# Two transformer blocks on one core: expert 0's first 512 inner columns for all tokens ahead of the routing, and a plan with four 64-row experts

## The chip, the cores and the metric

One core of a Trainium2 chip runs the whole program in one launch. The metric is the device time of one execution in microseconds, as the median of the runs; nothing is split over cores, so there is no slowest core to pick. The other quantities are those of one profiled execution.

## The reference

256 tokens of 1024 values go through two layers of one block and two of another, in float32. The part that matters here is the mixture of experts in the second layer of the first block:

```python
def moe_ffn(x, router_w, w1, w3, w2):
    logits = (xt @ router_w).astype(F32)                  # 256 x 8
    top_v, top_i = lax.top_k(logits, TOP_K)               # 2 of 8
    top_w = jax.nn.softmax(top_v, axis=-1)
    gates = jnp.sum(jax.nn.one_hot(top_i, N_EXPERTS, dtype=F32) * top_w[..., None], axis=1)
    for e in range(N_EXPERTS):
        y = y + gates[:, e:e + 1].astype(x.dtype) * swiglu(xt, w1[e], w3[e], w2[e])
```

`swiglu` is `(silu(x @ w1) * (x @ w3)) @ w2`, with 3584 inner columns for each expert. `x` is the output of a layer norm behind the projection `w_out` of the layer's mixer; behind the experts stands another layer norm with the residual `ALPHA * x`. The kernel computes an expert only for the tokens that were routed to it.

## The kernel before

**Weights.** Every weight comes in units of 1 MB, 128 partitions by 2048 values (`unit`, L169). SP issues the transfer into a tile `raw`; ScalarE writes the rounded high part `wh` and VectorE the rest `wl` (`split`, L165); TensorE multiplies high by high, high by low and low by high parts. There are four buffers each of `wh` and `wl`. `raw` has four of its own, and within the experts every third load takes one of the ten large buffers (`roomy`, L175).

**Routing.** `route` (L805) makes the logits, marks each token's two experts (`sel`), counts the tokens of each expert, sorts the experts by count into slots 0 to 7, and writes the experts' numbers, and a flag for the plan, as integers into `idi` (L883 to L889). SP reads the numbers from there, since they select the weights' addresses (L1154, L1233), and every engine reads the flag and branches (L1234 to L1239). Until then no expert's weight is fetched.

**Tiles.** The tokens of a slot are gathered by a product with a one-hot matrix into a tile `ring` (`place`, `gather`): 128 rows with high and low part in two halves, three matmuls for a product, or 64 rows with high and low part side by side in one stationary tile, two matmuls for a product. The plan `few` holds where slot 0 has at most 192 tokens, slot 1 at most 128 and slot 6 at most 64. It runs four groups: slot 0 with a 128-row and a 64-row tile together with slots 7 and 6 as 64-row tiles; slot 1; slots 2 and 3; slots 4 and 5. All of the last five have one 128-row tile.

**Steps.** An expert is done in seven steps f of 512 inner columns (`expert`, L931): two units of w1 and two of w3 (`up`), the product of the two (`gate`, `mul`), its transposition (`turn`), and two units of w2 (`down`). `phases` (L1160) writes the order by hand: in a step the experts of a round follow one another, and the `down` of an expert comes after the `up` of the next, so that `turn` has time. `stream` (L1068) issues the units two ahead of their use. The 128-row and two-tile experts sum over all seven steps in PSUM; the 64-row experts beside the two-tile expert, for which PSUM has no room, add each step's result to a tile `ysum` on VectorE (`add`, L1021). At the end `put_back` and `finish` bring the rows back to their tokens by a product with the transposed one-hot matrix (`sct`) and add them, times the gate, to the result (L1060). A 64-row gate takes ScalarE and VectorE in turn: a copy (L975), an add (L976), two activations (L977, L978).

**Order of instructions.** Each engine runs its own instructions in order. A scheduler sets that order when the program is built, from the order in which the code issues them and from what is ready; what stands inside a branch isn't mixed with what stands outside. In the projection ahead of the experts (`project`, L383) the last three units are run for token tile 0 and then for tile 1, and the layer norm of tile 0 (`post`) lies beside tile 1's products.

## Time and profile before

| | |
|---|---|
| median of 3 runs | 2357.88 us (2356.47 to 2361.75) |
| the profiled execution | 2355.55 us |
| its span, first to last instruction | 2353.8 us |
| TensorE busy | 2272.1 us, 97% of the span |
| VectorE busy | 1765.4 us, 75% |
| ScalarE busy | 1396.0 us, 59% |
| weight units of the experts | 336 transfers of 1024 KB |

A matmul is entered as busy until its modelled end, and the next one begins before that end; so a busy TensorE is a TensorE that was never without work, and the pace of its matmuls is read from their starts. The profile names the engines PE (TensorE; PEld are its weight loads), DVE (VectorE), ACT (ScalarE), POOL (GpSimd) and SP. `wl<-raw,wh` is VectorE's split of a unit, `wh<-raw` is ScalarE's, `lin` is the accumulator of w1 or w3, `y` that of w2, `uT` the transposed product, `ga` the gather.

### The profile page before, as it was taken

The numbers are of one execution on the slowest core, as the hardware profiler recorded it, in microseconds if no ns is written. First come the engines' busy times: TensorE is split into PE (matmuls) and PEld (weight loads), VectorE is DVE, ScalarE is ACT, GpSimd is POOL, SyncE is SP. The second block draws the span as 40 slices with busy tenths as digits, with TensorE's granted clock in tenths as the row PEclk, the third lists the DMA queues.
The fourth block names the chain that finished last, engine by engine and source line by source line (L and its number), as shares of the span: only waits on it lengthen the run. The fifth ranks groups of instructions, "written<-read, shape, count | busy, mean of one in ns | idle before, by whom it ended". The sixth has DMA issues, their size and how long they took to land. (4 is left out here: it accounts for less than half of the span.)

```text
span 2353.8 us, 29770 instructions
## 1 busy us (share of the span) xinstructions
PE 2272.1 (97%) x11444; PEld 1853.7 (79%) x11444; DVE 1765.4 (75%) x1907; ACT 1396.0 (59%) x1532; POOL 108.9 (5%) x154
## 2 busy tenths in 40 slices
PE   7999999799999989999999997999999999999998
PEld 6788887577777768888888886787888888888887
DVE  4665476798888998889888888897666459956653
ACT  5554354677777777676776765457555343764542
POOL 2100011000000000000000001000200001010000
PEclk9999999899999999999999999999999999999999
DMA  9556560699999999999999997643755553555552
GB/s 298 167 191 187 178 209 21 248 343 345 344 337 322 330 326 368 347 368 362 371 342 371 369 365 255 200 162 117 230 190 181 192 189 126 188 172 186 191 185 72
DMA packets 266968, 585.10 MB, mean 249 GB/s; under 512 B 10514, under 2 KB 21190, under 8 KB 266561
## 3 DMA queue, kind: packets, MB, share of 16 engines
q1 hardware_dynamic: 260880, 565.48, 68.4%
q0 software_dynamic: 5936, 17.64, 2.6%
q8 instruction: 91, 1.49, 0.3%
q14 instruction: 61, 0.49, 0.1%
HBM read 580.43 MB, written 2.64 MB: 248 GB/s over the span
## 5 line engine op out<-in xcount | busy, mean ns | idle before, releaser
L167 DVE TENSOR_TENSOR wl<-raw,wh 128x2048 fp32r<-128x2048 f32 (+2 forms) x532 | 1195.5, 2268 | 373.2 <-ACT wh L166 372.1
L166 ACT ACTIVATE wh<-raw 128x2048 fp32r<-128x2048 f32 (+2 forms) x532 | 990.2, 1891 | 383.8 <-PE lin L84 145.3
L950 PE MATMUL lin<-wh,ring 128*128 128x512 f32 x1680 | 556.0, 391 | 0.0
L950 PE MATMUL lin<-wl,ring 128*128 128x512 f32 (+1 forms) x1008 | 396.2, 393 | 3.7 <-DVE wl L167 3.3
L950 PEld LDWEIGHTS lin<-wh,ring 128*128 128x128 f32 x1680 | 315.4, 188 | 81.8
L950 PEld LDWEIGHTS lin<-wl,ring 128*128 128x128 f32 (+1 forms) x1008 | 171.4, 170 | 48.7 <-DVE wl L167 8.5
L84 PE MATMUL lin<-wh,hh 128*128 128x512 f32 x352 | 141.8, 403 | 0.0
L84 PE MATMUL lin<-wl,hh 128*128 128x512 f32 x352 | 138.4, 393 | 2.3 <-DVE wl L167 2.3
L84 PE MATMUL lin<-wh,hl 128*128 128x512 f32 x352 | 137.9, 393 | 0.1
L950 PE MATMUL y<-wl,uh 128*128 128x512 f32 x336 | 107.3, 400 | 3.4 <-DVE wl L167 3.4
L1442 DVE SCALAR_TENSOR_TENSOR ro<-conv,ro 128x256 f32<-128x256 f32 x240 | 105.4, 474 | 0.4
L950 PE MATMUL y<-wh,ul 128*128 128x512 f32 x336 | 104.2, 391 | 0.0
L950 PE MATMUL y<-wh,uh 128*128 128x512 f32 x336 | 104.1, 390 | 0.0
L84 PE MATMUL lin<-wh,h2h 128*128 128x512 f32 x256 | 101.1, 395 | 0.0
L84 PE MATMUL lin<-wl,h2h 128*128 128x512 f32 x256 | 99.9, 390 | 0.2
L84 PE MATMUL lin<-wh,h2l 128*128 128x512 f32 x256 | 99.3, 390 | 0.2
L84 PE MATMUL lin<-wh,xah 128*128 128x512 f32 (+1 forms) x240 | 87.4, 365 | 0.7 <-ACT xah L166 0.6
L84 PE MATMUL lin<-wl,xah 128*128 128x512 f32 (+1 forms) x240 | 86.6, 361 | 0.0
L84 PE MATMUL lin<-wh,xal 128*128 128x512 f32 (+1 forms) x240 | 86.4, 363 | 0.0
L166 ACT ACTIVATE uh<-uT 128x512 fp32r<-128x512 f32 x42 | 25.1, 598 | 99.3 <-PE uT L1004 99.3
L84 PEld LDWEIGHTS lin<-wl,hh 128*128 128x128 f32 x352 | 66.7, 190 | 16.1 <-DVE wl L167 3.2
L84 PEld LDWEIGHTS lin<-wh,hh 128*128 128x128 f32 x352 | 66.8, 190 | 15.6 <-issue 1.3
(548 smaller groups left out, 3812.5 us busy)
## 6 DMA issues: line engine op xcount, KB each, us to landing
raw<-in_moe_w SPq DMA_DIRECT2D x336, 1024.0 KB, 7.2
raw<-in_w_in SPq DMA_DIRECT2D x70, 1024.0 KB, 5.1
raw<-in_w_ff SPq DMA_DIRECT2D x64, 1024.0 KB, 5.2
raw<-in_ffn_w SPq DMA_DIRECT2D x32, 1024.0 KB, 5.1
raw<-in_w_out SPq DMA_DIRECT2D x12, 1024.0 KB, 8.0
raw<-in_w_branch SPq DMA_DIRECT2D x8, 1024.0 KB, 5.7
raw<-in_w_out SPq DMA_DIRECT2D x8, 512.0 KB, 7.4
raw<-in_w_branch SPq DMA_DIRECT2D x8, 512.0 KB, 6.3
```

Of the source, the lines that this page charges most:

```text
L84: nc.tensor.matmul(o, lhsT=lhsT, rhs=rhs, start=(self.i == 0 and self.fresh), stop=(self.i == self.n - 1), skip_group_check=True)
L166: self.nc.scalar.activation(h, src, AF.Copy)
L167: self.nc.vector.tensor_sub(l, src, h.bitcast(F32))
L950: nc.tensor.matmul(a.ap[:rows], lhsT=lhsT, rhs=u[part][:, kk, cs], start=(a.i == 0), stop=(a.i == a.n - 1), skip_group_check=True)
L1442: nc.vector.scalar_tensor_tensor(acc[:, f], uT[:, f, k:k + 256], cw[:, f, k:k + 1], acc[:, f], op0=OP.mult, op1=OP.add)
```

## The change

Expert 0 always gets slot 0 (1024 is added to its count before the sort). Its first step is done for all 256 tokens, without gathering (`everyone`): the first unit is issued within the projection (`hook`), and the products are issued between the parts of the routing, whose code is cut in two by a `yield`. The result is added to the output times expert 0's gate, which is 0 for tokens not routed to it. Expert 0's own round then has the six steps 1 to 6, on one 128-row tile, and the four w1 and w3 units of step 1 are issued ahead of the branch (`landed`). The raw tiles are a ring of six, four small ones and two of the large buffers.

There are three plans. `light` runs where slot 0 has at most 128 tokens, slot 1 at most 192, slot 2 at most 128, and slots 4 and 6 at most 64. Its groups are slot 0; slot 1 with two tiles together with slots 7, 6 and 5 as 64-row tiles (the third of their sums takes one raw tile of the ring until that expert is finished); slot 2; and slot 3 with 128 rows together with slot 4 with 64 rows, as two experts of one round, slot 4 summing in PSUM. `few` is what runs where only slot 4's limit fails.

```diff
@@ -166,19 +167,26 @@
+    def raw(self):
+        if self.raws:
+            self.raws.append(self.raws.pop(0))
+            return self.raws[-1]
+        return self.pw.tile([128, 2048], F32, tag="raw", name="raw")
...
-        self.loads += 1
-        raw = (self.big("raw") if self.roomy and self.loads % 3 == 0 else
-               self.pw.tile([128, 2048], F32, tag="raw", name="raw"))
+        there = bool(self.landed)
+        raw = self.landed.pop(0) if there else self.raw()
...
-        if layout == "rows":
+        if there:
+            pass
+        elif layout == "rows":
@@ -396,6 +404,8 @@
         self.warm(AF.Sqrt, x(orders[-1][-1], 1)[0])
         after = {t: (lambda t=t: post(t, [banks[0][t], banks[1][t]])) for t in range(2)}
         after[1, 1] = self.early
+        if self.hook:
+            after[0, 0] = self.hook
         yield from self.run_b(specs[cut:], x, tmajor=True, after=after)
@@ -761,15 +771,18 @@
+            if l == 1:
+                everyone = self.everyone(*(io[k][0, 0] for k in ("moe_w1", "moe_w3", "moe_w2")))
+                self.hook = everyone["first"]
             xt, tr1 = self.ln_out(self.mix1(l, xt, tr1), io["ln1_g"][l], io["ln1_b"][l])
+            self.hook = None
...
-                tr1()
-                self.moe(xt, io["router_w"][0], io["moe_w1"][0], io["moe_w3"][0], io["moe_w2"][0],
+                self.moe(xt, tr1, everyone, io["router_w"][0], io["moe_w1"][0], io["moe_w3"][0], io["moe_w2"][0],
                          io["ln2_g"][l], io["ln2_b"][l])
@@ -851,6 +864,7 @@
             nc.vector.tensor_scalar(sel[:, 8 * t:8 * t + 8], rank[:, 8 * t:8 * t + 8], 1.5, None, op0=OP.is_lt)
+        yield
         pc = self.bank("cum")
@@ -860,8 +874,11 @@
+        key = col(8)
+        nc.vector.tensor_copy(key, cnt)
+        nc.vector.tensor_scalar(key[:, 0:1], cnt[:, 0:1], 1024.0, None, op0=OP.add)
+        mine = key[:, :, None].to_broadcast([128, 8, 8])
+        other = key[:, None, :].to_broadcast([128, 8, 8])
...
+        most = (self.cap, self.cap + 64, self.cap, 64)
+        for i, (slot, m) in enumerate(zip((0, 1, 2, 6), most)):
+            if i == 0:
+                nc.vector.tensor_scalar(fit[:, 0:1], cs[:, 0:1], m + 0.5, None, op0=OP.is_lt)
+            else:
+                nc.vector.tensor_scalar(fit[:, i:i + 1], cs[:, slot:slot + 1], m + 0.5, fit[:, i - 1:i], op0=OP.is_lt,
+                                        op1=OP.mult)
+        nc.vector.tensor_scalar(fit[:, 4:5], cs[:, 4:5], 64.5, fit[:, 3:4], op0=OP.is_lt, op1=OP.mult)
+        nc.vector.tensor_add(fit[:, 5:6], fit[:, 3:4], fit[:, 4:5])
+        nc.vector.tensor_copy(idi[:, 16:17], fit[:, 5:6])
@@ -1012,8 +1035,8 @@
-                        if q == 0 and (f == 0 or inner):
-                            st[i]["y"] = [Acc(self.bank("y"), (4 if inner else 28) * per[i]) for c in range(2)]
+                        if q == 0 and (f == first or inner):
+                            st[i]["y"] = [Acc(self.bank("y"), (4 if inner else 28 - 4 * first) * per[i]) for c in range(2)]
@@ -1086,16 +1110,89 @@
+    def everyone(self, w1, w3, w2):
+
+        nc = self.nc
+        w = {"a": w1, "b": w3}
+        u, p, s, y, xt = {}, {}, {}, {}, []
+
+        def load(name, q):
+            u[name, q] = self.unit(w[name], list(range(4 * q, 4 * q + 4)), 0, 512)
+
+        def up(name, t):
+            x = self.xt_tok(xt)
+            p[name, t] = Acc(self.bank("lin"), 24)
+            for q in range(2):
+                h, l = u[name, q]
+                for kk in range(4):
+                    xh, xl = x(4 * q + kk, t)
+                    p[name, t].mm(nc, xh, h[:, kk])
+                    p[name, t].mm(nc, xh, l[:, kk])
+                    p[name, t].mm(nc, xl, h[:, kk])
+            if name == "a":
+                s[t] = self.mid("sa")
+                nc.scalar.activation(s[t], p[name, t].ap, AF.Silu)
+            else:
+                nc.vector.tensor_mul(s[t], s[t], p[name, t].ap)
+
+        def turn(t):
+            b = self.bank("uT")
+            for j in range(4):
+                nc.tensor.transpose(b[:, j * 128:(j + 1) * 128], s[t][:, j * 128:(j + 1) * 128], self.ident)
+            h, l = self.mid("uh", (128, 4, 128), dt=F32R), self.mid("ul", (128, 4, 128), dt=F32R)
+            self.split(h, l, b.rearrange("p (j c) -> p j c", c=128))
+            s[t] = h, l
+
+        def down(q):
+            h, l = self.unit(w2, [2 * q, 2 * q + 1], 0, 1024)
+            for t in range(2):
+                if q == 0:
...
+                    uh, ul = (z[:, 2 * q + kk] for z in s[t])
+                    for st, m in ((uh, h), (uh, l), (ul, h)):
+                        for c in range(2):
+                            y[t][c].mm(nc, st, m[:, kk, c * 512:(c + 1) * 512])
+
+        return dict(first=lambda: load("a", 0), load=load, up=up, turn=turn, down=down, y=y, xt=xt)
+
+    def moe(self, xt, tr1, everyone, rw, w1, w3, w2, g2, b2):
         tc, nc = self.tc, self.nc
-        gate, pos, iota, idi = self.route(xt, rw)
+        load, up, turn = (everyone[k] for k in ("load", "up", "turn"))
+        everyone["xt"].extend(xt)
+        self.raws = [*(self.raw() for _ in range(4)), self.big("raw"), self.big("raw")]
+        load("a", 1)
+        up("a", 0)
+        tr1()
+        route = self.route(xt, rw)
+        next(route)
+        load("b", 0)
+        load("b", 1)
+        up("b", 0)
+        up("a", 1)
+        gate, pos, iota, idi = next(route)
         xh = self.bigr("xh").rearrange("p (t d) -> p t d", d=D)
         xl = self.bigr("xl").rearrange("p (t d) -> p t d", d=D)
         acc = self.x
+        turn(0)
+        up("b", 1)
         for t in range(2):
             nc.scalar.activation(xh[:, t], acc[:, t], AF.Copy)
             nc.gpsimd.tensor_sub(xl[:, t], acc[:, t], xh[:, t].bitcast(F32))
             nc.scalar.activation(acc[:, t], acc[:, t], AF.Copy, scale=self.alpha)
+        turn(1)
+        for q in range(2):
+            everyone["down"](q)
+        for t in range(2):
+            for c in range(2):
+                o = acc[:, t, c * 512:(c + 1) * 512]
+                nc.vector.scalar_tensor_tensor(o, everyone["y"][t][c].ap, gate[t][:, 0:1], o, op0=OP.mult, op1=OP.add)
+        landed = []
+        for w in (w1, w3):
+            for q in range(2):
+                landed.append(self.raw())
+                nc.sync.dma_start(landed[-1].rearrange("p (k n) -> p k n", n=512),
+                                  w[0, 512 * q:512 * q + 512, 512:1024].rearrange("(k p) n -> p k n", p=128))
         ring = [self.bigr("ring") for _ in range(4)]
         ysum = self.big("ysum").rearrange("p (i d) -> p i d", d=D)
         for z in (*ring, ysum[:, 0], ysum[:, 1]):
@@ -1147,8 +1244,12 @@
             return tiles, lambda: self.gather(g, parts, xh, xl)
 
         index = {}
+        raws = list(self.raws)
+        sums = [ysum[:, 0], ysum[:, 1], raws[-1][:, 0:1024]]
 
         def weights(s):
+            if s == 0:
@@ -1163,7 +1264,7 @@
             for make, early, late in rounds:
                 es = make()
-                for f in range(7):
+                for f in range(es[0][5], 7):
                     for e in es:
                         jobs = e[0](f)
...
             yield call(e[4])
-            yield from e[1](6)
+            jobs = e[1](6)
+            yield jobs[0]
+            if done:
+                yield call(done[3])
+            yield from jobs[1:]
             yield call(e[3])
         def run(plan):
+            self.landed, self.raws = list(landed), list(raws)
...
                                 if inner is not None:
-                                    zs[0]["sum"] = ysum[:, inner]
-                                es.append(self.expert(zs, weights(s), acc))
+                                    zs[0]["sum"] = sums[inner]
+                                if inner == 2:
+
+                                    self.raws.remove(raws[-1])
+                                    zs[0]["free"] = lambda: self.raws.append(raws[-1])
+                                es.append(self.expert(zs, weights(s), acc, int(s == 0)))
@@ -1223,21 +1332,28 @@
-        few = [([(0, 0, False), (0, self.cap, True), (7, 0, True), (6, 0, True)],
-                [[(0, (0, 1), None), (7, (2,), 0), (6, (3,), 1)]])]
-        few += [([(1, 0, False)], [one(1)])]
-        few += [([(s, 0, False), (s + 1, 0, False)], [one(s), one(s + 1, 1)]) for s in (2, 4)]
-        many = [([(s, 0, False), (s, self.cap, False)], [[(s, (0, 1), None)]]) for s in range(3)]
-        many += [([(s, 0, False), (s + 1, 0, False)], [one(s), one(s + 1, 1)]) for s in (3, 5)]
-        many += [([(7, 0, False)], [one(7)])]
-        index[0] = nc.values_load(idi[0:1, 0:1], engines=[mybir.EngineType.SP], min_val=0, max_val=7)
-        n = nc.values_load(idi[0:1, 16:17], min_val=0, max_val=1)
-        self.roomy = True
-        with tc.If(n > 0) as cmp:
-            run(few)
+        light = [([(0, 0, False)], [one(0)]),
+                 ([(1, 0, False), (1, self.cap, True), (7, 0, True), (6, 0, True), (5, 0, True)],
+                  [[(1, (0, 1), None), (7, (2,), 0), (6, (3,), 1), (5, (4,), 2)]]),
+                 ([(2, 0, False)], [one(2)]),
+                 ([(3, 0, False), (4, 0, True)], [[(3, (0,), None), (4, (1,), None)]])]
+        few = [([(0, 0, False)], [one(0)]),
+               ([(1, 0, False), (1, self.cap, True), (7, 0, True), (6, 0, True)],
+                [[(1, (0, 1), None), (7, (2,), 0), (6, (3,), 1)]]),
+               ([(2, 0, False)], [one(2)]),
+               ([(3, 0, False), (4, 0, False)], [one(3), one(4, 1)]),
+               ([(5, 0, False)], [one(5)])]
+        many = [([(s, 0, False), (s, self.cap, False)], [[(s, (0, 1), None)]]) for s in range(4)]
+        many += [([(s, 0, False), (s + 1, 0, False)], [one(s), one(s + 1, 1)]) for s in (4, 6)]
+        n = nc.values_load(idi[0:1, 16:17], min_val=0, max_val=2)
+        with tc.If(n > 1) as cmp:
+            run(light)
         with cmp.Else():
-            run(many)
-        self.roomy = False
+            with tc.If(n > 0) as inner:
+                run(few)
+            with inner.Else():
+                run(many)
+        self.raws = []
```

## Rows read from the trace of the kernel before

**Rows 1.** The page, DMA in 40 slices of 58.8 us (busy tenths).

```profile
DMA  9556560699999999999999997643755553555552
```

**Rows 2.** Stretches: us, then busy us (instructions) of PE, PEld, DVE, ACT, POOL; clock, DMA share, GB/s.

```profile
547.95:603.37 55.42, 53.72 (x245) 39.66 (x245) 48.96 (x34) 40.73 (x33) 0.00 (x0) 1.00 0.97 342
...
1396.19:1412.97 16.78, 16.78 (x78) 13.87 (x77) 14.68 (x9) 12.01 (x9) 0.00 (x0) 1.00 1.01 371
```

**Rows 3.** Waits, 480 to 820 us: who waits for whom, total us, times, longest.

```profile
DVE wl L167 <- ACT wh L166: 29.8, 35, 1.8
...
PE y L950 <- DVE wl L167: 6.1, 14, 0.8
...
PE lin L950 <- DVE wl L167: 1.7, 4, 0.6
```

**Rows 4.** Waits, 840 to 1400 us.

```profile
ACT wh L166 <- PE lin L950: 10.5, 15, 2.5
...
PE lin L950 <- DVE wl L167: 1.0, 1, 1.0
```

**Rows 5.** Groups by line, VectorE, 547.95 to 603.37 us: busy us, mean ns, idle before.

```profile
L167 DVE TENSOR_TENSOR wl<-raw,wh 128x2048 fp32r<-128x2048 f32 x18 | 40.8, 2287 | 4.9 <-ACT wh L166 4.7
...
L1029 DVE TENSOR_TENSOR ysum<-ysum,y 128x512 f32<-128x512 f32 x5 | 3.2, 680 | 0.0
...
L985 DVE TENSOR_TENSOR sa<-sa,lin 128x512 f32<-128x512 f32 x4 | 2.7, 680 | 1.4 <-PE lin L950 1.4
...
L976 DVE TENSOR_TENSOR sa<-lin,sa 64x512 f32<-64x512 f32 x3 | 2.0, 682 | 0.1
...
L167 DVE TENSOR_TENSOR uhl<-uT,uhl 128x256 fp32r<-128x256 f32 x3 | 1.3, 419 | 0.1
```

**Rows 6.** Timeline of TensorE in one step of the two-tile round: start us, duration.

```profile
547.95 0.50 PE L950 MATMUL lin<-wl,ring 128*128 128x512 f32 x1 [0.38 <-DVE wl L167]
...
566.14 0.39 PE L950 MATMUL y<-wh,uhl 128*128 128x512 f32 x1
...
569.82 0.60 PE L1004 MATMUL uT<-ident,sa 128*128 128x128 f32 x4
...
571.10 0.47 PE L950 MATMUL lin<-wh,ring 128*128 128x512 f32 x1
...
578.59 0.62 PE L950 MATMUL y<-wh,uh 128*128 128x512 f32 x2
...
588.33 1.00 PE L997 MATMUL uT<-keep,sa 128*128 128x64 f32 x8
...
589.14 0.47 PE L950 MATMUL lin<-wh,ring 128*128 128x512 f32 x1
...
603.37 0.50 PE L950 MATMUL lin<-wl,ring 128*128 128x512 f32 x1 [0.37 <-DVE wl L167]
```

**Rows 7.** Timeline between projection and experts, TensorE and VectorE.

```profile
411.30 0.39 PE L84 MATMUL prj<-wh,yl 128*128 128x512 f32 x1
...
431.47 0.29 DVE L1124 TENSOR_SCALAR g<-keep 128x128 fp32r<-128x128 f32 x1 [0.52 <-DVE keep L879]
...
441.97 0.39 PE L950 MATMUL lin<-wh,ring 128*128 128x512 f32 x1
```

**Rows 8.** Stretches from the projection's end on.

```profile
411.90:424.20 12.30, 4.91 (x42) 4.34 (x42) 9.56 (x30) 6.11 (x9) 3.83 (x8) 0.79 0.00 1
424.20:433.30 9.10, 1.90 (x9) 1.83 (x9) 6.41 (x41) 0.00 (x0) 0.00 (x0) 0.50 0.04 7
433.30:442.00 8.70, 8.70 (x33) 7.10 (x34) 5.43 (x21) 6.38 (x23) 0.00 (x0) 0.84 1.03 378
...
442.00:461.00 19.00, 18.42 (x81) 13.95 (x79) 16.61 (x21) 15.57 (x24) 0.00 (x0) 1.00 1.04 393
...
835.00:1457.00 622.00, 616.22 (x2807) 506.74 (x2805) 551.87 (x365) 436.27 (x317) 1.87 (x4) 1.00 0.98 357
```

**Rows 9.** Groups by line, 470 to 880 us: the update of the result.

```profile
L1060 DVE SCALAR_TENSOR_TENSOR xn<-sct,keep,xn 128x512 f32<-128x512 f32 x12 | 8.3, 743 | 1.4 <-PE sct L84 1.4
```

20 lines of the change are left out of this document (9 added, 11 removed).

## The prediction

> **What bounds the kernel now.** I read four views: the page's slices, to find the stage that the change touches; the table by stretches, for the period of that stage; the waits, for the engine that ends it; and the groups by line, for the prices.
>
> The slices [rows 1] show the mixture of experts as the long run of nines in the DMA row, from the ninth to the twenty-fourth slice, about 940 us. Ahead of it stands a hole, the digit 0 of the seventh slice: nothing is fetched until the routing is known. One would take the nines for a stage bound by transfers. The stretches say otherwise. The stage has two kinds of step. While the two-tile expert and two 64-row experts run, a step (512 inner columns of each of the three, 18 weight units of 1 MB) takes 55.42 us, of which TensorE is busy 53.7 and VectorE 49.0 [rows 2]. While one 128-row expert runs, a step of 6 units takes 16.8 us, TensorE is busy in all of it, VectorE in 14.68 [rows 2]. In the waits of both stretches no row has the splits waiting for a transfer. TensorE waits for a split (wl) 7.8 us of 340 in the first and 1.0 of 560 in the second, where ScalarE in its turn waits for TensorE to free a weight buffer [rows 3, 4]. So TensorE is the bound, VectorE 10% behind it, and the transfers are there in time.
>
> The price that decides is that of a split. It costs VectorE 2.22 us a unit (14.68 less a product and the split of a turned tile, 0.68 each [rows 5], over 6) whatever the number of rows, while TensorE's price goes with the rows: 12 matmuls of a unit for 128 rows, 8 for 64.
>
> **Which plan runs.** From the reference with its default inputs the experts get 51, 28, 134, 12, 80, 48, 37 and 122 tokens. Before: the two-tile expert is 2, beside it 1 and 3 with 64 rows, then five 128-row experts (7, 4, 0, 5, 6). After, slot 0 is expert 0 (51, limit 128), slot 1 has 134 (192), slot 2 has 122 (128), slot 4 has 48 (64), slot 6 has 28 (64): all limits hold, the flag is 2 and the plan `light` runs. Expert 6 goes from 128 rows to 64 beside the two-tile expert, expert 5 to 64 beside expert 4, and expert 0 loses one of its seven steps.
>
> **The change part by part.** Four terms.
>
> *A, the head.* Before, the last product of the projection starts at 411.30 and the first of the experts at 441.97 [rows 7]; between them TensorE is busy 4.9, 1.9 and 8.7 us, and the clock granted is 0.79, 0.50 and 0.84 [rows 8]. After, expert 0's first 512 columns for all 256 rows stand in between: 144 matmuls of 0.227 us (80 from 547.95 to 566.14 [rows 6]), 32.8 us. Add the routing's 6.8 and twice four transposes, at most 1.2 (0.60 each, 569.82 [rows 6]): TensorE ends at 452.5. Then come, with TensorE idle, the last two updates of the result on VectorE (0.74 each [rows 9]), the branch (0.52, VectorE's idle time at 431.47 [rows 7]) and two one-hot tiles with their clearing, about 0.9 (0.29 each [rows 7]); then the gather, with 256 columns in place of 512, half of 8.7. That makes 459.8 with no stall, some 457 where the routing's matmuls no longer run at the halved clock. For stalls I add 3.5 to this: 460.5, so **+18.5 us**. If none of the six splits (13.3 of VectorE) lay beside matmuls it would be 470, +28.5; I stay near the lower end, since TensorE has 32.8 us of other work in that stretch. The ends are +15 and +28.5. The ten transfers (six of expert 0, four ahead for its second step) are issued on SP before any wait on the routing, in the hole, and cost nothing; the new routing instructions (five, of some 0.2) lie beside the matmuls. POOL's clearing of the last ring tiles waits until the transposed activations are freed, since two big tiles more are held; nobody needs these before the gather.
>
> *B, expert 0 has six steps left:* **-16.8** [rows 2]. The prefetch of its units adds nothing to this, as no step waits for transfers.
>
> *C, expert 6 beside the two-tile expert.* Seven steps of 16.8 go, and the step of 55.42 becomes longer by X. For TensorE X is 12.0: 32 matmuls from 571.10 to 578.59, 16 from 566.14 to 569.82, and 0.8 for the turn, 588.33 to 589.14 [rows 6]. For VectorE it is 16.4: six splits, 13.3, and an add, a product, a split of the turned tile and two additions to the sum, 3.1 [rows 5]. VectorE's free 6.4 us of the present step do not absorb that: they lie in the stretch where TensorE is slow on two tiles and all four weight buffers are full, while at the end of the 64-row stretch TensorE already waits for a split (0.37 at 603.37 [rows 6]), so no lead is left there. The added expert comes exactly at this place and runs at VectorE's pace. I take X = 16.2, a little under VectorE's price. 7 x (16.2 - 16.8) = **-4**. Ends: X = 12.6, if VectorE's free time took up the difference and TensorE kept its present waits, gives -29; X = 18.4, VectorE's price and 2 us in which ScalarE's copy of a 64-row gate waits for TensorE with the next split queued behind it, gives +11. One raw buffer fewer in this round (five for six) I cost at nothing, as the step needs 24 units in 71.6 us, 2.98 each, and the fetch gives one in 2.67 [rows 8].
>
> *D, expert 5 beside expert 4.* Two steps of 16.8 become one of 12 units: TensorE 28.8, VectorE 14.7 + 15.1 = 29.8, the fetch 12 x 2.67 = 32.0 (393 GB/s, the fastest stretch of the stage [rows 8]). So here the transfers become the bound. I take 33.0 for the step: 7 x (33.0 - 33.6) = **-4**, with ends of -11 (32.0) and +7 (34.6, splits that wait as in C).
>
> *Small terms.* One of the gathers inside the rounds now has 512 columns, +3; the added 64-row expert's return to the result takes VectorE some 5 us where VectorE is the bound instead of where it had room, and the last two experts end together, +2. **+5**, ends +2 and +8.
>
> Sum: 18.5 - 16.8 - 4 - 4 + 5 = -1.3. The profiled execution took 2355.55 with a span of 2353.8, and the median of the three runs is 2357.88, 2.33 above it; on the median the forecast is 2356.6, rounded to **2356**. What TensorE is spared, 264 of 4032 matmuls or 60 us, comes back in three places: in the head, in VectorE's splits, in the fetch.
>
> In D the row and a rule part. The stage's first stretch moves 393 GB/s, and the 128-row steps take a unit in 2.80 us, 374 GB/s, with TensorE and not the fetch at its limit [rows 2, 8]; by these D is -4. The Trainium skill (DMA: Bandwidth & Descriptors, "Where 436 GB/s comes from") holds that between HBM and SBUF the HBM share of a core, about 358 GB/s, is what binds; by that the step of D would be an estimated 35.1 us and the whole sum about +13 in place of -1.3.
>
> **The rivals.**
> 1. *Faster: VectorE's free time takes up the added splits.* For it: 6.4 us free in each step [rows 2]. Against: the four weight buffers are the only lead, and TensorE meets the 64-row stretch's end without any. X = 12.6 gives 25 us less than forecast, 2331. Chance 0.17.
> 2. *Slower: the in-order wait on ScalarE decides.* In the four-expert stretch each 64-row gate makes ScalarE wait for TensorE, and the split behind it is late for VectorE, which then has no lead to give (VectorE waited 29.8 us for ScalarE in 340 already [rows 3]). X = 18.4 gives 15 more, 2371. It decides once that round's step is over 73 us. Chance 0.18.
> 3. *The plan `light` doesn't run* (the counts are other than I work out). Then experts 5 and 6 stay alone with 128 rows: A and B stay, C and D fall away, one gather more: 18.5 - 16.8 + 9, 2368. Chance 0.03.
> 4. *The fetch can't go faster than its mean in the stage's second stretch,* 357 GB/s [rows 8], 2.94 us a unit. Then the single steps are 17.6 (seven of them, +6) and the step of D is 35.3 (+16): some 22 us more, 2378. The steps of 16.8 [rows 2] and the stretch with 393 GB/s speak against it. Chance 0.02. It is what the page cited above would have.
>
> **How the numbers follow.** The forecast has 0.57; by the ends of A, C and D its own range is 2345 to 2367. 0.2% is 4.7 us, about what a measurement of this kernel tells from no change, so "same" is 2353.2 to 2362.6, near half of the forecast's weight (0.28). Of its rest 0.17 lies below and 0.12 above. Faster: 0.17 + 0.17 and 0.02 of what I have not thought of, 0.36. Same: 0.28 and 0.01 of the same, 0.29. Slower: 0.12 + 0.18 + 0.03 + 0.02, 0.35. The range of 8 in 10 goes from 2339 to 2374; outside are most of rival 1 and the far end of rivals 2 and 4.
>
> **What would show it.** A: the first `lin` product out of a `ring` tile at about 460, and TensorE busy from 411 to 450 with the DMA row no longer 0 there. B: six steps of 16.8 first. C: steps of about 71.6 with 24 splits, VectorE busy over 65, TensorE waiting for wl some 5 to 7 us a step where it waited 1.7; steps under 69 would prove me wrong and rival 1 right, over 73 rival 2. D: steps of 33 with ScalarE's splits waiting for raw transfers. If no 64-row turn stands in the last round, rival 3 holds.

## The result and the profile after

The changed kernel takes **2392.22 us** (median of 4 runs, 2391.97 to 2394.0), the kernel before 2357.71: a ratio of **1.0144** (95% interval 1.0128 to 1.016), 34.5 us slower. The forecast was 2356, with a range of 2339 to 2374. The profiled execution took 2394.0, with a span of 2392.2.

The page says first where to look: what TensorE is spared it now waits for. These are lines of the page, for the whole execution. A group's line gives busy us, mean ns, and the idle time just before with what ended it; the line by itself is the same group in the kernel before.

```profile
PE 2256.4 (94%) x11240; PEld 1798.3 (75%) x11240; DVE 1784.8 (75%) x1958; ACT 1421.2 (59%) x1568; POOL 109.2 (5%) x154
...
DMA  9455563497999999889999997553655554556552
...
L973 PE MATMUL lin<-wl,ring 128*128 128x512 f32 (+1 forms) x992 | 398.2, 401 | 46.8 <-DVE wl L168 45.8
```

```profile
L950 PE MATMUL lin<-wl,ring 128*128 128x512 f32 (+1 forms) x1008 | 396.2, 393 | 3.7 <-DVE wl L167 3.3
```

TensorE is busy 16 us less than before (2272.1), and the span is 38 longer. Ahead of products of `lin` with a `wl` it stood idle for 46.8 us, where the kernel before has 3.7. The seventh slice of the DMA row, a 0 in [rows 1], is a 3 now (and the 6 behind it a 4): the prefetch fills part of the hole.

The head is the stretch from the projection to the first product of the gathered experts (timeline of TensorE, as in [rows 7]; start, duration, what it waited for):

```profile
415.27 0.39 PE L84 MATMUL prj<-wh,yl 128*128 128x512 f32 x1
...
425.90 0.45 PE L328 MATMUL tr<-ident,xn 128*128 128x128 f32 x1 [4.80 <-DVE xn L383]
...
450.41 0.65 PE L1141 MATMUL uT<-ident,sa 128*128 128x128 f32 x4 [0.78 <-DVE sa L1136]
...
463.88 0.35 PE L945 MATMUL ga<-g,xh 128*128 128x256 f32 x1 [1.90 <-DVE g L1243]
...
469.27 0.40 PE L973 MATMUL lin<-wh,ring 128*128 128x512 f32 x1
```

Two stretches of it, the second tile's transpositions with the routing's first products, and the gather (columns as in [rows 2]):

```profile
425.90:431.00 5.10, 5.05 (x42) 4.68 (x43) 2.77 (x8) 3.03 (x4) 2.48 (x2) 0.58 0.84 308
463.90:469.30 5.40, 5.40 (x33) 5.40 (x34) 3.72 (x3) 1.46 (x5) 0.00 (x0) 0.68 0.01 2
```

The last product of the projection is 4.0 us later than before, the first of the experts 27.3 (469.27 against 441.97).

The rounds, with the same columns: two steps of the two-tile round, one 128-row step, one step of the last round.

```profile
744.30:818.10 73.80, 68.34 (x303) 48.78 (x302) 65.17 (x45) 53.96 (x42) 0.00 (x0) 0.98 0.95 342
818.10:891.90 73.80, 67.10 (x303) 47.99 (x302) 65.20 (x46) 53.96 (x42) 0.00 (x0) 1.00 0.95 342
1143.50:1160.30 16.80, 16.80 (x77) 13.91 (x76) 16.67 (x10) 12.51 (x8) 0.00 (x0) 1.00 1.03 389
...
1317.30:1352.30 35.00, 30.40 (x134) 22.17 (x133) 29.69 (x18) 25.21 (x18) 0.00 (x0) 1.00 0.99 345
```

In the two-tile step no engine is full: 73.8 us with TensorE busy 67 to 68, VectorE 65, ScalarE 54; so too in the last round (35.0 with 30.4, 29.7, 25.2). That suggests engines that wait for one another in turn. Who waits for whom (total us, times, longest), first in one two-tile step:

```profile
ACT sa L998 <- PE lin L973: 7.2, 3, 3.7
DVE wl L168 <- ACT wh L167: 6.8, 7, 1.8
...
ACT uhl L167 <- PE uT L1020: 5.9, 3, 3.2
PE lin L973 <- DVE wl L168: 4.0, 4, 1.8
ACT sa L1003 <- PE lin L973: 3.1, 1, 3.1
```

and in one step of the last round:

```profile
...
DVE wl L168 <- ACT wh L167: 4.3, 4, 1.3
PE lin L973 <- DVE wl L168: 2.9, 3, 1.8
ACT sa L998 <- PE lin L973: 2.9, 1, 2.9
ACT uhl L167 <- PE uT L1020: 2.7, 1, 2.7
```

It is a circle: ScalarE's gates and turned tiles (`sa`, `uhl`) wait for TensorE, VectorE's splits for ScalarE's, TensorE for VectorE's. No transfer stands in either list, nor in the part of it not shown. Where the circle closes is seen in ScalarE's timeline in the last round, first at the gate of the 64-row expert, with the product of TensorE that meets the lateness:

```profile
1318.38 3.71 ACT L167 ACTIVATE wh<-raw 128x2048 fp32r<-128x2048 f32 x2
1324.98 0.59 ACT L998 ACTIVATE sa<-lin 64x512 f32<-64x512 f32 x1 [2.88 <-PE lin L973]
1325.60 1.92 ACT L167 ACTIVATE wh<-raw 128x2048 fp32r<-128x2048 f32 x1
```

```profile
1329.89 0.44 PE L973 MATMUL lin<-wl,ring 128*64 128x512 f32 x1 [1.82 <-DVE wl L168]
```

Two splits end at 1322.1, and then the gate waits 2.9 us for TensorE's product. The split queued behind the gate starts at 1325.6, although TensorE had last used its buffer at 1319.7. VectorE's half follows at 1327.55 and ends at 1329.8, and TensorE, which had waited 1.8 us for it, goes on at 1329.9. The gate of the 128-row expert does the same:

```profile
1337.19 5.53 ACT L167 ACTIVATE wh<-raw 128x2048 fp32r<-128x2048 f32 x3
1344.72 0.60 ACT L1003 ACTIVATE sa<-lin 128x512 f32<-128x512 f32 x1 [2.00 <-PE lin L973]
1345.21 5.52 ACT L167 ACTIVATE wh<-raw 128x2048 fp32r<-128x2048 f32 x3
```

Three splits come first, then the gate, which waits until TensorE has finished its second unit at 1344.7, then three splits more. The first of these needs the buffer of the first unit, whose last product starts at 1341.6: it could have begun at 1342.7, right behind the third, but stood 2.5 us behind the gate. VectorE's lead shrinks by that, and TensorE runs out of it in a step's 64-row stretch, where it uses up a unit in 1.9 us and VectorE makes one in 2.2 (in the step shown it waits 0.37, 0.72 and 1.82 us at 1320.3, 1323.1 and 1329.9).

**The ledger**, profiled execution against profiled execution, from the starts of the turns and the first and last products: head +27.3; expert 0's step -16.8; two-tile round 7 x (73.8 - 55.42 - 16.8) = +11.1; last round 7 x (35.0 - 33.6) = +9.8. The remainder, +2.7, is what is left for gathers, finishing and steps that differ from the usual (the first two-tile step takes 72.2). The last `sct` then ends 34.1 us later (1490.0 against 1455.9). Another 4.3 of the span's 38.4 come behind the stage, which the change doesn't touch.

### The profile page after: what moved, and what is told of

It is laid out like the page before. It is cut to its first block, busy times and chain, and to the rows that moved or that the text cites. A ratio compares the mean times of both kernels' runs of the same rounds, so it can differ in the third digit from the quotient of the medians.

```text
span 2392.2 us, 29365 instructions
## 1 busy us (share of the span) xinstructions
PE 2256.4 (94%) x11240; PEld 1798.3 (75%) x11240; DVE 1784.8 (75%) x1958; ACT 1421.2 (59%) x1568; POOL 109.2 (5%) x154
## 5 line engine op out<-in xcount | busy, mean ns | idle before, releaser
L973 PE MATMUL lin<-wh,ring 128*128 128x512 f32 x1424 | 497.7, 396 | 3.1 <-ACT wh L167 2.7
L973 PE MATMUL lin<-wl,ring 128*128 128x512 f32 (+1 forms) x992 | 398.2, 401 | 46.8 <-DVE wl L168 45.8
L973 PEld LDWEIGHTS lin<-wh,ring 128*128 128x128 f32 x1424 | 269.5, 189 | 88.2 <-ACT wh L167 8.8
L973 PEld LDWEIGHTS lin<-wl,ring 128*128 128x128 f32 (+1 forms) x992 | 157.8, 159 | 109.7 <-DVE wl L168 70.5
L84 PE MATMUL lin<-wh,xah 128*128 128x512 f32 (+1 forms) x272 | 100.4, 370 | 0.7 <-ACT xah L167 0.6
L973 PE MATMUL y<-wl,uhl 128*64 128x512 f32 x280 | 90.4, 404 | 10.5 <-DVE wl L168 10.4
L84 PE MATMUL lin<-wl,xah 128*128 128x512 f32 (+1 forms) x272 | 99.3, 365 | 0.0
L84 PE MATMUL lin<-wh,xal 128*128 128x512 f32 (+1 forms) x272 | 99.0, 366 | 0.0
L973 PE MATMUL y<-wh,uhl 128*128 128x512 f32 x280 | 89.3, 400 | 0.0
L84 PEld LDWEIGHTS lin<-wh,hl 128*128 128x128 f32 x352 | 66.3, 188 | 15.2 <-DVE hl L168 0.9
L973 PE MATMUL y<-wl,uh 128*128 128x512 f32 x216 | 70.0, 406 | 6.8 <-DVE wl L168 6.8
```

Source lines behind the costliest of these rows:

```text
L84: nc.tensor.matmul(o, lhsT=lhsT, rhs=rhs, start=(self.i == 0 and self.fresh), stop=(self.i == self.n - 1), skip_group_check=True)
L973: nc.tensor.matmul(a.ap[:rows], lhsT=lhsT, rhs=u[part][:, kk, cs], start=(a.i == 0), stop=(a.i == a.n - 1), skip_group_check=True)
```

## The experiments

Steps are distances between turns of a round's first expert. Kernels are edits of the changed kernel unless something else is said, and the diffs show the parts that matter (three dots stand for what lies between). A ratio is to the runs of the kernel before that were taken beside the experiment, with its 95% interval.

**The parts apart.** First the head runs without the new plan (the flag is capped):

```diff
-        nc.vector.tensor_add(fit[:, 5:6], fit[:, 3:4], fit[:, 4:5])
+        nc.vector.tensor_copy(fit[:, 5:6], fit[:, 3:4])
```

> The flag is capped at 1, so that expert 0 still comes first, but the plan has three rounds as before: experts 5 and 6 with 128 rows, seven steps of 16.8 each. This is A and B alone. Theory 1 (the first expert product comes at about 469, 27 us later than before, and not at the forecast 460.5): 2357.7 + 27 - 16.8 and one gather more of some 3, 2368 to 2372. Rival (the head costs the forecast 18.5 and the rest is lost in the rounds): 2360 to 2364.

Measured: 2378.77, ratio 1.0095 (1.0075 to 1.0116), 7 above the upper end of theory 1. The two-tile step is 55.4 again. The first expert product comes at 472.2, so that the head costs 30.2 here and not 27 (the gather waited 4.4 us for its one-hot tile, 1.9 in the changed kernel), and 7.4 are left for the fifth round and its gather, where 3 were expected.

Then the plan runs without the head:

```diff
-                self.hook = everyone["first"]
...
-            if s == 0:
-                return [w[0] for w in (w1, w3, w2)]
...
-                                es.append(self.expert(zs, weights(s), acc, int(s == 0)))
+                                es.append(self.expert(zs, weights(s), acc, 0))
```

(Expert 0 also loses its fixed place in the slots, and its work in the head isn't issued. The rounds are the two-tile expert with slots 7, 6 and 5; slot 1; slots 2 and 4; slot 3.)

> Expert 0 is an expert like the others again (seven steps, after the routing), the plan with four 64-row experts stays. This is C and D alone. Theory 1 (the step with three 64-row experts is 73.8 and the step with one beside a 128-row expert 35.0, both as in the changed kernel): C +11, D +10, gathers and finishing +3, 2380 to 2384. Rival (the forecast's terms, the changed kernel's steps being long only because of what came ahead of them): 2352 to 2358.

Measured: 2384.26, 1.0112 (1.0091 to 1.0133). The steps are 73.8 and 35.0 without any head ahead of them, so the plan makes them long. **Both parts lose by themselves.** Added up (22.8 and 28.3 above the kernel before beside them, 2355.95) they would give 51 us, not 34.5. Each of the two kernels has costs of its own: the first the fifth round and gather, the second a projection whose last product starts 5.7 us later than in the kernel before, with TensorE's clock at half (last section).

**The rounds: whose order?** First, each gate, product and split of a turned tile on ScalarE and VectorE is put behind the splits:

```diff
-    def stream(self, jobs, ahead=2):
+    def stream(self, jobs, ahead=3):
...
+        def behind(f, *args):
+            a, b = self.newest
+            with self.tc.issue_after(a), self.tc.issue_after(b):
+                f(*args)
...
-            then()
+            behind(then)
```

> The same work in the same buffers, but three units are looked ahead and each gate, product and split of a turned tile on ScalarE and VectorE is put behind the split of the newest of them, so that a split whose buffer is free no longer stands behind an instruction that waits for TensorE. Theory 1 (the steps are long because of that order, rival 2 of the prediction): the steps of the last round fall from 35.0 to 33 or less, those of the two-tile round from 73.8 to 71.5 or less, in all 2355 to 2368. Rival A (VectorE's work itself sets the step): the two-tile step stays over 73. Rival B (the fetch, 12 units at 358 GB/s): the step of the last round stays at 35, the two-tile step falls; 2372 to 2380.

Measured: 2385.29, 1.0122 (1.0099 to 1.0145), far above theory 1's range. The steps of the last round fall to 30.5, 30.5, 31.0, 31.9 and 32.2. The first of them:

```profile
1295.80:1326.30 30.50, 29.23 (x133) 22.34 (x132) 29.49 (x18) 25.49 (x19) 0.00 (x0) 1.00 1.05 394
```

It has the same 12 units, matmuls and splits. Theory 1 holds there, and rival B is out: the same transfers go through in 30.5 us. But the two-tile step rose to 74.0 to 75.6, which by the expectation's words speaks for rival A. TensorE's waits tell of another cause: it waited for banks (2.0 a step behind `raw<-raw,y`) and for products (4.0) that now stood behind splits on VectorE. The next run decides between them.

Only ScalarE's queue is ordered now, in the changed kernel, in the plan alone, and in the kernel before (the lines with a minus are those of the run above):

```diff
-            a, b = self.newest
-            with self.tc.issue_after(a), self.tc.issue_after(b):
+            with self.tc.issue_after(self.newest[0]):
```

> As the run with the splits first, but only ScalarE's queue is ordered so; VectorE keeps the order it had. In that run the last round's step fell to 30.5 while the two-tile step rose to 74 to 75.6, with TensorE waiting 5.9 us a step for banks that VectorE's sums and products, now behind splits, freed late. Theory 1 (the stall of the changed kernel is on ScalarE alone, VectorE's new waits were of that run's own making): last round 30.5 to 31.5, two-tile step 70 to 72, in all 2340 to 2355. Rival (VectorE's price of 16.4 for the added expert sets the two-tile step whatever ScalarE does): two-tile step 73 or more, in all 2358 to 2366.

Measured: 2362.98, 1.0013 (1.0003 to 1.0022): 29 us below the changed kernel without any work less. The two-tile step is 70.2, as theory 1 had it, so rival A is out. The last round, 32.1, is above theory 1's 31.5. The total lies 8 above theory 1 and in the rival's range, for two reasons outside these steps: the first turn comes 18.0 us behind the first expert product (12.1 in the changed kernel), and a change of round got longer (84 where it was 81).

```profile
744.80:815.00 70.20, 66.33 (x301) 47.91 (x300) 64.88 (x45) 54.09 (x42) 0.00 (x0) 1.00 1.00 358
1334.60:1366.70 32.10, 30.39 (x133) 22.08 (x132) 29.50 (x18) 25.65 (x18) 0.00 (x0) 1.00 1.04 393
```

All runs with such an order in the rounds, these and those that follow, also look three units ahead instead of two, and no run has that alone. So a step of theirs against one of the changed kernel shows order and lookahead together; between two ordered runs it shows order alone.

> The plan with four 64-row experts alone (expert 0 not first) together with ScalarE's queue in that order. Theory 1: the same steps as in the run before this one of the call (30.5 to 31.5 and 70 to 72) without what the head costs and without a step saved, 28 to 45 us below the plan alone: 2335 to 2356, so about the kernel before or better. Rival (VectorE sets the two-tile step): 2356 to 2362.

Measured: 2356.88, 0.9988 (0.9978 to 0.9999), even with the kernel before. The total is 1 above theory 1 and in the rival's range, but the steps, 70.2 and 32.1, are not the rival's.

> The kernel before with ScalarE's queue in that order, nothing else changed: what the order alone is worth where no 64-row expert stands beside a 128-row one. TensorE's waits for splits there are 1.3 us of a two-tile step of 55.4 and 0.03 of a single step, so at most 9 us: 2348 to 2358. If it gains more than 12, the order and not the plan is what a faster version owes its time to.

Measured: 2373.69, 1.0064 (1.0041 to 1.0088), 15 slower, where I had expected a small gain or none. The order is no gift: here it puts the gathers' copies behind splits too (the first gather takes 14.7 us for 8.8) and lengthens the two-tile round by 9. Of the two plans it paid only in the one with four 64-row experts. So it was narrowed to gates and turns, on both engines, in the plan alone, three units ahead (`behind` issues its first argument behind the instructions named after it):

```diff
-            return [(*job("a", w1, 0, 0), none), (*job("a", w1, 1, 0), gate),
+            return [(*job("a", w1, 0, 0), none), (*job("a", w1, 1, 0), lambda: self.behind(gate, *self.newest)),
...
-                        yield call(lambda e=e, f=f: e[2](f))
+                        yield call(lambda e=e, f=f: self.behind(lambda: e[2](f), *self.newest))
```

> The plan alone, three units looked ahead, and only gates and turns put behind the newest split, on ScalarE and VectorE; products, sums, gathers and finishing stay as the scheduler has them. Theory 1 (what stalled TensorE was gates and turns ahead of splits; what the two earlier orders lost was sums and products behind splits, and gathers and finishing at the rounds' changes): two-tile step 69 to 71, the step with one 64-row expert 30.5 to 31.5, changes of round as in the plan alone, in all 2328 to 2342, faster than the kernel before. Rival (the bound moves to VectorE's own work and the changes): 2350 to 2358.

Measured: 2352.36, 0.9973 (0.9963 to 0.9982), in the rival's range. The two-tile step is 70.2, as theory 1 had it, the last round 32.1, not 30.5. Next the products too are put behind the splits, in the round of a 128-row and a 64-row expert:

```diff
-                    (*job("b", w3, 0, 0), none), (*job("b", w3, 1, 0), mul)]
+                    (*job("b", w3, 0, 0), none),
+                    (*job("b", w3, 1, 0), (lambda: self.behind(mul, *self.newest)) if tiles[0].get("pair") else mul)]
...
+                                zs[0]["pair"] = len(r) == 2
```

> The plan alone with gates and turns in order, and in the round with one 64-row expert beside a 128-row one the products too. Theory 1: that round's step goes from 32.1 to 30.5 to 31, in all 8 to 11 us below the run with gates and turns alone, 2341 to 2345. Rival (the 30.5 came from the orders of sums, gathers and finishing): the step stays at 32, 2350 to 2354.

Measured: **2346.13, 0.9948 (0.9931 to 0.9965), faster than both kernels**. Four of the seven steps take 30.5 to 31.5. That is the whole of D: 35.0, less 2.9 by gates and turns (with the lookahead), less 1.6 by the product, an edit of order alone.

What is left in the two-tile step? The next kernel leaves out VectorE's splits for the added expert, so that the low parts of its weights are missing:

```diff
+        elif layout == "high":
+            self.newest = nc.scalar.activation(h[:, :m], raw[:, :m], AF.Copy).ins, self.newest[1]
+            return hv, hv
```

> The plan alone with gates and turns in order, but the added 64-row expert of the two-tile round goes without the low halves of its weights: 42 subtractions of VectorE are left out, the high half is used in their place, TensorE's work is the same. Theory 1 (what is left above TensorE's 67 us in that step is VectorE's work): the step falls from 70.2 to 66.5 to 68. Rival (waits of another kind, the raw buffers or the product of the two-tile gate): 69.5 or more.

Measured: 2325.26, with a step of

```profile
601.20:670.20 69.00, 65.81 (x301) 48.07 (x300) 51.98 (x39) 54.74 (x43) 0.00 (x0) 1.00 1.00 365
```

Thirteen us of VectorE's work gone (65.0 to 52.0) shorten the step by 1.2, between the two expectations. VectorE's load is not what sets it. TensorE is busy 65.8 of the 69.0, and what holds the rest is not shown. Some 22 us lie between this profiled execution and that of the run with gates and turns: about 10 in these steps and 13 behind the last of them, up to the first turn of the round of slots 2 and 4, where VectorE finishes four experts among the splits. That was not taken further.

> The plan alone with gates and turns in order, and five 64-row experts in three rounds: the 134-token expert with three of them, the 80-token one alone, the 122-token one with two. Theory 1: the last round's step is 32.1 and 14.5 to 15.5 for the second 64-row expert, 46.5 to 47.5, in place of 32.1 and a single step of 16.8, and one round less: 10 to 20 us below the run with gates and turns alone, 2332 to 2342. Rival (with two added experts VectorE's 16.4 each decides, 49 or more): within 4 us of that run.

In this kernel the last round's third sum lies in the buffer of the norm's gain and bias and overwrites them; its work is that of a kernel with a buffer more. Measured: 2347.74, 0.995 (0.9934 to 0.9966), 5 below the run with four, between theory 1 and the rival. The step is 48.4 with VectorE busy 45.8: 16.3 for the second added expert, about VectorE's price of 16.4. That VectorE sets it is a reading from these two numbers, no run takes its work away.

The same fifth expert was also tried in another place, the expert with 51 tokens as a 64-row one beside the expert with 122. Expected were 14 to 25 us less than with four, or, as the rival, within 5. Measured: 2341.97, 0.9922 (0.9904 to 0.994), 10 less, between the two, with steps of 32.1 in that round. But as its code reads, the second round's gather writes a tile that the two-tile expert still uses, so it does not do the work of the others, and its time doesn't show a gain.

**The head.** The first try moves the first split in the code:

```diff
-                self.hook = everyone["first"]
...
+        load("a", 0)
         load("a", 1)
```

> Expert 0's first unit is fetched and split behind the projection with its second, not between the projection's two row tiles. Theory 1 (that split is queued on VectorE ahead of the attention's last splits and costs the projection 4 us): the projection's end moves back to about 412 and the whole becomes 2 to 4 us faster, 2388 to 2390. Rival (the split is in VectorE's way wherever it stands, now in the layer norm): 2391 to 2395, no change or a little slower.

Measured: 2395.16, 1.0167 (1.0145 to 1.0188), but inconclusive: the edit did not move the split, which still stands inside the attention on both engines (ScalarE at 390.38 and VectorE at 392.51, in the changed kernel 391.24 and 393.39). Then by force (`yl` is VectorE's last split of the attention, `xn_in` the last instruction of the second tile's norm):

```diff
-            u[name, q] = self.unit(w[name], list(range(4 * q, 4 * q + 4)), 0, 512)
+            with self.tc.issue_after(self.xn_in if name == "b" else self.yl):
+                u[name, q] = self.unit(w[name], list(range(4 * q, 4 * q + 4)), 0, 512)
```

> The changed kernel, but on VectorE the split of expert 0's first unit is put behind the attention's last split and those of its third and fourth unit behind the layer norm of the second row tile. Theory 1 (three splits of 2.3 us in VectorE's queue ahead of that layer norm delay the transposes and so the routing): the transposes of the second tile come 4 to 7 us earlier, the first expert product at 461 to 465 instead of 469, in all 2385 to 2389. Rival (the head is bound by TensorE's own work): no change, 2391 to 2394.

Measured: 2394.34, 1.0153 (1.013 to 1.0175): no change, the rival's time. But the wait for the second tile's norm went as theory 1 expected (4.8 to 0.3), and another took its place:

```profile
PE lgT L852 <- DVE rwhl L168: 4.3, 1, 4.3
PE ga L947 <- DVE g L1246: 1.9, 1, 1.9
```

The split of the router's weights, 0.2 us elsewhere, was now late. Next the marks are set on both engines, and moved to the splits of the second tile (`xs`) and of the router's weights (`rs`); the line with a minus is that of the run above:

```diff
-            with self.tc.issue_after(self.xn_in if name == "b" else self.yl):
+            marks = (*self.xs, *self.rs) if name == "b" else self.ys
```

> The changed kernel with the splits of the head placed on both engines: expert 0's first unit behind the attention's last split (in the run before, ScalarE's half of it still stood ahead of a copy in the attention and the projection ended 2.4 us late), its third and fourth behind the splits of the second row tile and of the router's weights (there TensorE waited 4.3 us for the latter). Theory 1 (the head's loss against the forecast is made of these two): projection ends at 411.5 to 412, first expert product at 459 to 462, in all 2383 to 2387. Rival (another wait takes their place, as in the run before): first product at 464 or later, 2388 to 2392.

Measured: 2398.78, 1.016 (1.0135 to 1.0186), 7 above even the rival's range, with the first expert product at 474.1. As the rival had it, another wait took the old one's place: TensorE waits 4.0 for the router's split again (ScalarE does a copy of the residual, a table load and expert 0's gate ahead of it) and 3.7 for the routing's own copies. Is it work rather than order? The next kernel leaves out VectorE's six splits in the head, so that the low parts of those weights are missing:

```diff
+            self.high = True
             u[name, q] = self.unit(w[name], list(range(4 * q, 4 * q + 4)), 0, 512)
+            self.high = False
```

> The changed kernel without the low halves of expert 0's first six units (its first 512 inner columns): ScalarE's copies stay, VectorE's six subtractions (2.28 each) are left out and the high half is used in their place, the matmuls are the same in number. Theory 1 (VectorE's splits in the layer norm and the routing are the head's extra): TensorE's wait of 4.8 for the second tile's norm falls to under 1.5 and the first expert product comes 47 to 50 us behind the projection's end, where the forecast had 48.8 and the changed kernel has 54. Rival (ScalarE's and TensorE's own chain): 52 or more.

Measured: 2389.29. The norm's wait is gone, yet the first expert product comes 51.8 us behind the projection's last (54.0 in the changed kernel), between the two expectations and next to the rival's 52. TensorE waits 4.1 for the router's split, which ScalarE makes late. So ScalarE's order was tried (parts of the edit):

```diff
-        up("a", 0)
         tr1()
         route = self.route(xt, rw)
         next(route)
+        up("a", 0)
...
-                nc.scalar.activation(s[t], p[name, t].ap, AF.Silu)
+                self.behind(lambda: nc.scalar.activation(s[t], p[name, t].ap, AF.Silu), *self.xs, *self.rs)
```

> The changed kernel with the routing's chain first: expert 0's first unit behind the attention's last split, its first gate and the residual's copies behind the second tile's and the router's splits, its third and fourth unit behind the choice of experts. The same work. Theory 1 (the head's loss is order on ScalarE and VectorE): no wait of TensorE over 2.5 us ahead of the router's products, first expert product 48 to 50 us behind the projection's end (54 in the changed kernel, 48.8 forecast), in all 2384 to 2389. Rival (TensorE's part of 48.8 was too low, or the third and fourth unit now come late): 52 or more, 2390 to 2396.

Measured: 2394.15, 1.0152 (1.0131 to 1.0173), with 53.2 us between the two products: the rival. The router's split is in time, but TensorE waits 4.7 for the norm again, since expert 0's first product no longer stands in that hole. With it put back, and the rounds in the order of the fastest kernel:

> The whole change with the routing's chain first and expert 0's first product back in the hole ahead of the second tile's transposes, and in the rounds gates and turns behind the newest split, in the last round the products too. Theory 1 (order on ScalarE and VectorE explains all three stalls): first expert product 46 to 49 us behind the projection's end, two-tile step 70.2, last round's step 30.5 to 31.5; the head then costs 16 to 19 us and the step saved gives 16.8, so that the whole comes within 8 us of the plan alone in the same order (2346): 2342 to 2354. Rival (the head keeps its loss whatever the order): first product at 51 or more, 2356 to 2368.

Measured: 2369.37, 1.0041 (1.0027 to 1.0055), 1 above the rival's range. The rounds hold (70.2, 30.5 to 31.9); the head is the rival's, 57.5 us:

```profile
PE uT L1151 <- DVE sa L1146: 9.0, 2, 8.2
PE ga L953 <- DVE g L1255: 1.9, 1, 1.9
```

Both old waits are gone, and expert 0's gate, put off behind the routing, is now 8.2 us late.

The whole change was also run with the head of the second try by force and gates and turns in order in the rounds. Expected were 2326 to 2345, or, as the rival, 2352 to 2362. Measured: 2371.93, 1.0055 (1.0033 to 1.0076), above both. Its steps are the ordered ones, 70.2 and 32.1; the head takes 57.4 us, and changes of round up to 85.8.

Over all these kernels the distance in the head was 52 to 58 us. Kernels that leave the head's code as it is spread as widely (54.0 in the changed kernel, 57.7 with the flag capped, 52.65 with the rounds in order), so differences of 3 or 4 us between orders say little. Whether some order comes to the forecast's 49 stays open.

## Why the prediction was wrong

**A, the head:** forecast +18.5, measured 27.3, a term mis-sized by 8.8. From the projection's last product to the experts' first it was 30.7 us before; the forecast's 460.5 meant 49.2, and it is 54.0. That is 4.8 of the 8.8. The other 4.0 lie ahead: TensorE is already 2.1 late at 366 us, far from the change (the clock granted from 100 to 150 us was 0.97 here and 1.00 before), another 1.0 goes where the clock was 0.83, from 375 to 385, and 1.0 is the change's: ScalarE's half of the first unit stands in the attention, between the last two transpositions of `oT` (7.1 us apart, 6.0 before).

The step that failed is "for stalls I add 3.5", together with the 2.8 taken off for the clock (457 in place of 459.8). The stalls are 4.8 and 0.8, and the clock granted was 0.58 in the routing's first products and 0.68 in the gather all the same. The sum without stalls, 48.5 behind the projection's last product, and 5.6 of stalls make the 54.0. I had counted TensorE's 32.8 us right and taken its cover for granted; but ScalarE and VectorE, which carry the norm and the routing, got three splits, two table loads and a gate more around the projection's end, ahead of the second tile's norm. That these splits make the wait for the norm is shown: it is 0.3 with them behind the norm and gone without them. That the head would be shorter for it is not: each time another wait took its place, so what would bring the head to 49 is open. "If none of the six splits lay beside matmuls" was the wrong bound to ask for: they did lie beside matmuls, and in front of the norm.

**B:** right. Six steps of 16.8 follow, -16.8.

**C, the two-tile round:** forecast X = 16.2, measured 73.8 - 55.4 = 18.4. That is rival 2 (chance 0.18), price and place: steps over 73, and no lead left at the 64-row stretch. Its mechanism is seen in the timeline, and with ScalarE's splits ahead of its gates and turned tiles (and three units of lookahead) X is 14.8. The step that failed is "it runs at VectorE's pace". VectorE's 16.4 was neither floor nor ceiling: with the order mended X is below it, without 13 us of VectorE's work it is 13.6, near TensorE's price plus its old waits (12.6, my lower end). I had put rival 2's 2 us on top of VectorE's price as a far end; the row that should have raised it stood in [rows 3], 29.8 us of VectorE waiting for ScalarE, nearly five a step, in a round with two 64-row gates. With three they are 6.8 a step.

**D, the last round:** forecast 33.0, measured 35.0. The failing step is "so here the transfers become the bound". They did not: 35.0 is the same circle, and with gates, turns and products behind the splits (and three units of lookahead) it is 30.5. The forecast's floor of 32.0, from 2.67 us a unit, was none. In the step of 30.5 TensorE is busy 29.2 and VectorE 29.3, and ScalarE's waits for transfers, 2.0 us, head its list; which of these bounds it is not shown. I gave D an end of +7 for "splits that wait as in C" and did not use it. The Trainium skill (DMA: Bandwidth & Descriptors, "Where 436 GB/s comes from") holds that the HBM share of a core, about 358 GB/s, binds, from which the prediction estimated 35.1 us. The trace shows 35.0, and yet the page explains nothing here: in 30.5 us the same twelve units came in at 394 GB/s. A number that fits is not yet a cause; the waits of that stretch, without one transfer, had said so. By that rule the step of D alone would have come out, for a wrong reason; the sum it gave, about +13, was not the measured one either. Rival 4 is out with its 0.02.

**Small terms:** +5 forecast; the remainder of the ledger is +2.7. Rival 1 (VectorE's free time absorbs the splits) is nearer the truth for an ordered queue (X = 14.8) than for this one. Rival 3 did not happen: the 64-row turns stand in the last round.

By the forecast's terms the miss is 8.8 in A, 15.1 in C and 13.8 in D, less 2.3 of small ones: 35.4 up to the stage's last `sct`. The 4.3 behind the stage come on top. The bad ends of the prediction's own terms (28.5, 11, 7 and 8, less 16.8) add up to 2396 on the median; the range stopped at 2374, as if they would not come together, though C's and D's have one cause. So the mechanism of the main loss was among the rivals, and the forecast had put its weight on another.

## What to carry to other kernels

When work is made smaller on the bounding engine, ask which instructions of the other engines wait for that engine and what is queued behind them: ScalarE, busy 54 of 73.8 us, set the pace here because its queue held a ready split behind a gate that wasn't. The engines' prices alone didn't give the step; the circle of waits did, and the wait list of the kernel before hinted at it with 29.8 us of VectorE waiting for ScalarE. An order has to be tried where it is to be used: the same rule gave 29 us in this kernel and cost 15 in the one before.

## What the runs showed of the hardware

**A split on VectorE was longer beside a subtraction on POOL.** In the changed kernel, VectorE and POOL:

```profile
417.25 3.28 DVE L168 TENSOR_TENSOR wl<-raw,wh 128x2048 fp32r<-128x2048 f32 x1
```

```profile
415.98 2.40 POOL L1181 TENSOR_TENSOR xl<-xn,xh 128x1024 fp32r<-128x1024 f32 x1 [14.46 <-ACT xh L1180]
```

A split takes 2.28 elsewhere. This one was issued 1.1 us ahead of the end of POOL's subtraction (418.38) and took 1.0 longer; the router's split of 0.2 us took 1.62 in the run with VectorE's head order and ended with POOL's instruction. The norm's instructions with an operand in PSUM ran beside it at their usual 0.67. The Trainium skill (SBUF — State Buffer, "Who interferes with whom") describes one port pair that VectorE and GpSimd lock in turn; this trace agrees.

**The clock granted in one stretch differs from kernel to kernel.** The plan alone, 375 to 385 us, where the code is that of the kernel before:

```profile
375.00:385.00 10.00, 9.98 (x36) 5.08 (x34) 4.25 (x9) 2.28 (x9) 1.08 (x2) 0.50 0.31 91
```

TensorE was granted 0.50, its level of 1.2 GHz, all through it, after ten us in which it was busy for 9.3 at 0.99. The kernel before, busy 9.5 from 375 to 385, was granted 1.00 there, and so were thirteen of the eighteen experiments. The projection's last product then starts at 417.05, where three kernels with the same plan and 1.00 there have 411.8 to 411.9. These 5 us are as much as an edit of the head's order was expected to give, and what brings the fall on these runs do not tell.
